# The router's products as fp32r with high and low parts side by side, and the second norm written over the tile of the input tokens

## The chip, the cores and the metric

The kernel runs on one core of a Trainium2 chip. What counts is the device time in microseconds of one execution. Before the change it is 1837.02 us, the median of three runs (1834.33 to 1839.08).

## The reference, cut to what matters

One layer over 1024 tokens of 1024 features. After the token mixing, its output projection with the gated residual, the second norm and the choice of tokens by 16 experts follow:

```python
y_x = (sigmoid(ga) * a + sigmoid(gb) * bb) @ w_out
x = x + g1 * y_x
h = modulate(rms_norm(x, norm2_g), sh2, sc2)          # (..)*(1+sc2) + sh2
aff = softmax((h @ w_router).astype(float32), axis=-1) # 1024 x 16
gate, idx = top_k(swapaxes(aff, 1, 2), 128)            # per expert: its 128 best tokens
xe = h[idx]                                            # gathered for each expert
```

Then each expert computes silu(xe @ w_gate) * (xe @ w_up) @ w_down for its 128 tokens, and a final norm closes. All is float32, and the choice of tokens depends on small differences in aff.

## The kernel before

Most products are done with operands that are split into a high part (rounded to fp32r) and a low part (the rest); three fp32r products, high x high, low x high and high x low, stand for one float32 product. `split` (L90 to L93) makes the two: a cast on ACT (L92), then a subtraction on DVE (L93). A few products are plain float32, the router's among them.

The stages follow each other: norms and the projection w_in, the scan, attention, the merge of the branches, the output projection with second norm and router (about 1079 to 1191 us), the search for the 128 best tokens per expert (to about 1216), the experts, the final norm. TensorE's (PE's) instructions run in the order in which the code writes them. DVE, ACT, POOL and the SP queue, which issues most DMAs, have their order from a scheduler that goes by due times and by `tc.high_priority`. Each engine's instructions run in their order, so one that waits holds up all that stand behind it.

The output projection works on eight tiles t of 128 tokens, each in four column quarters c of 256. For one (t, c) `y_mm` issues 24 fp32r products into the PSUM tile py. After two quarters `y_part` follows: x1 = py * g1 (L1083, DVE), x1 += xin, the input tokens (L1084, DVE), the squares' sum (L1085, ACT, which writes its unused elementwise result over xin). After the last quarter x1 goes to ACC, POOL computes the root r (L1089 to L1093), and `second_norm` writes h = x1 * r * s2 (L1100, DVE), adds sh2 (L1101) and sends h to the DRAM tensor H (L1102, SP), from which the experts gather. h has one buffer, xin two, x1 three, hT one.

The router doesn't read h: the norm's gain is multiplied into wr beforehand (`head2`, L968 to L973, in the merge stage), and r and the shift's part c0 are applied to the products. `x1_turn` transposes half of x1 (four blocks of 128x128) into pth and copies it to hT (L1109, ACT for the first half of a tile, DVE for the second). `router` runs eight float32 products of hT and wr, which have hT as weights and 16 columns (L1115), and the softmax's first steps (re, L1119; the maximum, L1120; exp, L1122; the reciprocal, L1123), raised in priority. `spread` scales into affb (ACT, L1133), transposes it (PE, L1135) and copies it to ar and aff.

For the last tiles `y_mm` and these small steps are interleaved by hand: `after` appends steps to the deque `turns`, and the table TN tells how many are taken behind each y_mm. So router(3) comes directly behind the transposes of its second half, router(5) as well, while router(0), (1), (2), (4) and (6) have one y_mm between; spread comes one or more y_mm behind its router. After the last y_mm TensorE has only the last transposes, router(7) and spread(7), and then the small products of the search.

pth, plg (the router's PSUM tile) and psp (spread's) share two PSUM banks. The tile aux, which POOL fills for the search (L1199 to L1206), has its own place.

Of the kernel before, what the change touches and what calls it, by code (L numbers as in the profile page):

```python
# [16 lines left out]
OP = mybir.AluOpType  # L17
# [4 lines left out]
D = 1024  # L22
# [23 lines left out]
def _layer(tc, nc, top, A, out):  # L46
# [9 lines left out]
    rt = top.enter_context(mkpool(name="rt", bufs=1))  # L56
# [185 lines left out]
    with ExitStack() as st:  # L242
        pool = st.enter_context(mkpool("right", name="pre", bufs=1))
        ps = st.enter_context(mkpool(name="preps", bufs=1, space=PSUM))
# [72 lines left out]
        for k in range(8):  # L317
            w2 = hx_pool.tile([128, 2, 2048], F32R, name="wm2", tag="hx1%d" % (k % 2))
            split(w2[:, 0], w2[:, 1], wm[k])
            for j in range(4):  # L320
                for i in range(2):
                    nc.tensor.matmul(pm[j], s4[:, k], w2[:, i, j * 512:(j + 1) * 512],
                                     start=(k == 0 and i == 0), stop=(k == 7 and i == 1))
# [14 lines left out]
        for j in range(16):  # L338
# [7 lines left out]
                                       op0=OP.add, op1=OP.mult)  # L346
# [42 lines left out]
    with ExitStack() as st:  # L389
        pool = st.enter_context(mkpool("right", name="sa", bufs=2))  # L390
# [39 lines left out]
        with tc.high_priority(offset=LK):  # L430
# [6 lines left out]
            r = pool.tile([128, 20], F32, name="kr_", bufs=1)  # L437
# [93 lines left out]
    with ExitStack() as st:  # L531
        pool = st.enter_context(mkpool("right", name="hg", bufs=1))
# [415 lines left out]
    with ExitStack() as st:  # L948
# [9 lines left out]
        nc.sync.dma_start(hd[8:], dram(sMod, 1024, [[128, 16], [1, 128]]))  # L958
        cols = rt.tile([128, 24], F32, name="cols")
        c0 = rt.tile([128, 16], F32, name="c0")  # L960

        def head():
            pv = ps.tile([128, 512], F32, name="pvc", tag="pth")
# [4 lines left out]
        def head2():  # L968
            pc = ps.tile([128, 512], F32, name="pc0", tag="pth")
            for k in range(8):  # L970
                nc.tensor.matmul(pc[:, :16], cols[:, 8 + k:9 + k].to_broadcast([128, 128]), wr[:, k], start=(k == 0), stop=(k == 7))
            nc.vector.tensor_copy(c0, pc[:, :16])
            nc.vector.tensor_tensor(wr, wr, cols[:, 16:, None].to_broadcast([128, 8, 16]), op=OP.mult)  # L973


        MG = [[[mp.tile([128, 4, 512], F32R, name="mg", tag="mg%d%d%d" % (i, c, n)) for n in range(2)] for c in range(2)] for i in range(2)]
# [72 lines left out]
        n2 = pool.tile([128, D], F32, name="n2", tag="xin", bufs=2)  # L1049
        nc.sync.dma_start(n2, dram(A["norm2_g"], 0, [[0, 128], [1, D]]))  # L1050
        nc.vector.scalar_tensor_tensor(row["s2"], row["s2"], 1.0, n2, op0=OP.add, op1=OP.mult)
        mats = pool.tile([128, 2, 128], F32, name="mats", tag="h", bufs=1)
        nc.scalar.dma_start(mats, A["c_mats"])
        nc.gpsimd.tensor_copy(tri, mats[:, 0])
        nc.gpsimd.tensor_copy(blk, mats[:, 1])
# [13 lines left out]
        X1 = {}  # L1069

        def y_part(t, c, nc_):

            ts, cs = slice(t * 128, (t + 1) * 128), slice(c * 256, (c + nc_) * 256)
            if c == 0:
                x = pool.tile([128, D], F32, name="xin", tag="xin", bufs=2)
                nc.sync.dma_start(x, A["x"][0, ts])
                x1 = pool.tile([128, D], F32, name="x1", tag="x1", bufs=3)
                ss = pool.tile([128, 4], F32, name="ss2", bufs=2)
                hT = pool.tile([128, 8, 128], F32, name="hT", tag="hT", bufs=1)
                X1[t] = [x, x1, ss, hT]  # L1080
            x, x1, ss, _ = X1[t]
            p = PY[t, c, "both"] if nc_ == 2 else PY[t, c]
            nc.vector.tensor_tensor(x1[:, cs], p, row["g1"][:, cs], op=OP.mult)  # L1083
            nc.vector.tensor_tensor(x1[:, cs], x1[:, cs], x[:, cs], op=OP.add)  # L1084
            nc.scalar.activation(x[:, cs], x1[:, cs], AF.Square, scale=1.0 / 32, accum_out=ss[:, c:c + 1])  # L1085
            if c + nc_ == 4:
                nc.sync.dma_start(ACC[ts], x1)
                m = pool.tile([128, 1], F32, name="r2m", tag="r2m", bufs=2)
                nc.gpsimd.tensor_scalar(m, ss[:, :1], ss[:, 2:3], EPS, op0=OP.add, op1=OP.add)  # L1089
                if nc_ == 1:  # L1090
                    nc.gpsimd.tensor_scalar(m, m, ss[:, 3:4], None, op0=OP.add)
                r = pool.tile([128, 1], F32, name="r2", tag="r2", bufs=2)
                nc.gpsimd.tensor_tensor(r, m, mhalf[:, :1], op=OP.pow)  # L1093
                X1[t].append(r)
                if t < 7:
                    second_norm(t, x1, r)

        def second_norm(t, x1, r):
            h = pool.tile([128, D], F32, name="h", tag="h", bufs=1)
            nc.vector.scalar_tensor_tensor(h, x1, r, row["s2"], op0=OP.mult, op1=OP.mult)  # L1100
            nc.vector.tensor_tensor(h, h, row["sh2"], op=OP.add)  # L1101
            nc.sync.dma_start(H[t * 128:(t + 1) * 128], h)  # L1102

        def x1_turn(t, c, nc_):
            _, x1, _, hT, *_ = X1[t]
            p = ps.tile([128, 4, 128], F32, name="pth", tag="pth")[:, :2 * nc_]
            for k in range(2 * nc_):
                nc.tensor.transpose(p[:, k], x1[:, (2 * c + k) * 128:(2 * c + k + 1) * 128], ident)
            (nc.vector.tensor_copy if c == 2 else nc.scalar.copy)(hT[:, 2 * c:2 * c + 2 * nc_], p)  # L1109

        def router(t):
            _, x1, _, hT, r = X1.pop(t)
            p = ps.tile([128, 512], F32, name="plg", tag="pth")[:, :16]
            for k in range(8):
                nc.tensor.matmul(p, hT[:, k], wr[:, k], start=(k == 0), stop=(k == 7))  # L1115
            m = pool.tile([128, 4], F32, name="rm", tag="rm", bufs=2)
            e = pool.tile([128, 16], F32, name="re", tag="re", bufs=2)
            with tc.high_priority(offset=100):
                nc.vector.scalar_tensor_tensor(e, p, r, c0, op0=OP.mult, op1=OP.add)  # L1119
                nc.vector.tensor_reduce(m[:, 0:1], e, axis=AX.X, op=OP.max)  # L1120
                nc.vector.tensor_scalar(m[:, 1:2], m[:, 0:1], -1.0, None, op0=OP.mult)
                nc.scalar.activation(e, e, AF.Exp, bias=m[:, 1:2], scale=1.0, accum_out=m[:, 2:3])  # L1122
                nc.vector.reciprocal(m[:, 3:4], m[:, 2:3])  # L1123
            EM[t] = e, m, x1, r

        EM = {}

        def spread(t):

            ab = pool.tile([128, 16, 8], F32, name="affb", tag="affb")  # L1130
            with tc.high_priority(offset=100):
                e, m, x1, r = EM.pop(t)
                nc.scalar.activation(ab, e[:, :, None].to_broadcast([128, 16, 8]), AF.Copy, scale=m[:, 3:4])  # L1133
                p = ps.tile([128, 512], F32, name="psp", tag="pth")[:, :128]
                nc.tensor.transpose(p, ab.rearrange("p e r -> p (e r)"), ident)  # L1135
                nc.vector.tensor_copy(ar16[:, t * 128:(t + 1) * 128], p.bitcast(U16)[:, 1::2])
                nc.scalar.copy(ar[:, t * 128:(t + 1) * 128], p)
                nc.scalar.copy(aff[:, t], ab[:, :, 0])
            if t == 7:
                second_norm(t, x1, r)  # L1140

        for k in ((0, 6), (6, 8)):
            for t in range(2):
# [48 lines left out]

    CAP = 128
    pos = rt.tile([128, 16, 8], BF, name="pos")
    aux = rt.tile([128, 8, 16, 5], BF, name="aux")
    with ExitStack() as st:
        pool = st.enter_context(mkpool(name="tk", bufs=1))
        ps = st.enter_context(mkpool(name="tkps", bufs=1, space=PSUM))
# [312 lines left out]
```

## Time and profile before

| | us |
|---|---|
| median of three runs | 1837.02 |
| profiled execution | 1835.68 |
| its span | 1833.9 |
| PE busy in the span | 1728.6 (94%) |
| DVE busy | 1325.1 (72%) |
| ACT busy | 981.6 (54%) |
| POOL busy | 225.1 (12%) |

The profile is one execution, taken on the core. The span runs from its first to its last instruction; the run around it is 1.8 us longer. Busy shares are means over stages with different limits: what a change in one stage is worth is read from that stage, by the order in which each engine works and by what ends its waits. PE is a matmul, PEld the load of its weights, which runs beside the matmul before; a float32 product leaves two records of each, an fp32r one a single record. fp32r operands appear as f32 in PE's rows. SPq is the SP engine issuing a DMA; its duration is that of the issue, and the time to landing stands elsewhere. A row of the timeline with x16 merges 16 like instructions, from the first's start to the last's end.

### The profile page before, as it was taken

How to read it: one execution, taken by the hardware profiler on the slowest of the kernel's cores; microseconds unless marked ns; L12 is line 12 of the kernel's file. 1: busy time of each engine (PE TensorE's matmuls, PEld its weight loads, DVE VectorE, ACT ScalarE, POOL GpSimd, SP SyncE). 2: the span in 40 equal slices, each digit the busy share in tenths (PEclk: the TensorE clock that was granted, in tenths of full speed). 3: DMA queues.
4: the chain of work that ended last, by engine and by line, in shares of the span. 5: the costliest groups of instructions: out<-in, count | busy, mean ns of one | idle time of the engine just before them, and what ended most of it. 6: DMA issues, size and time to landing. Idle time of an engine off the chain costs nothing. (4 is left out here: it accounts for less than half of the span.)

```text
span 1833.9 us, 26101 instructions
## 1 busy us (share of the span) xinstructions
PE 1728.6 (94%) x9819; PEld 1451.0 (79%) x9820; DVE 1325.1 (72%) x2016; ACT 981.6 (54%) x1608; POOL 225.1 (12%) x218
## 2 busy tenths in 40 slices
PE   5899999999999899999999999849999999999996
PEld 2799887899988678787777899838888888887774
DVE  5756322876756567777887664469999999999897
ACT  6522331332322367777767432237777777776665
POOL 3400001020000201111100010030010011001103
PEclk8899999999999999999999999969999999999998
DMA  8386445353332311101222676569999999999962
GB/s 321 98 290 238 155 144 186 128 159 106 128 113 81 119 51 34 53 24 58 94 91 99 223 269 230 176 238 356 380 380 375 382 385 369 383 384 381 357 244 95
DMA packets 206319, 383.87 MB, mean 209 GB/s; under 512 B 17488, under 2 KB 65568, under 8 KB 202864
## 3 DMA queue, kind: packets, MB, share of 16 engines
q1 hardware_dynamic: 194944, 360.92, 55.2%
q0 software_dynamic: 4832, 19.34, 3.9%
q10 hardware_dynamic: 6416, 1.94, 0.4%
q8 instruction: 77, 1.26, 0.3%
q14 instruction: 50, 0.41, 0.1%
HBM read 323.02 MB, written 59.13 MB: 208 GB/s over the span
## 5 line engine op out<-in xcount | busy, mean ns | idle before, releaser
L93 DVE TENSOR_TENSOR elo<-eraw,ehi 128x1024 fp32r<-128x1024 f32 x378 | 452.1, 1220 | 22.4 <-ACT ehi L92 14.9
L92 ACT CAST ehi<-eraw 128x1024 fp32r<-128x1024 f32 x384 | 383.7, 1048 | 86.5 <-PE pgu L178 48.4
L177 PE MATMUL pgu<-elo,xeT 128*128 128x512 f32 x512 | 203.5, 397 | 2.8 <-DVE elo L93 2.4
L176 PE MATMUL pgu<-ehi,xeT 128*128 128x512 f32 x512 | 205.3, 401 | 0.2 <-ACT xeT L92 0.2
L178 PE MATMUL pgu<-ehi,xeT 128*128 128x512 f32 x512 | 201.6, 394 | 0.0
L176 PE MATMUL pj<-hx,whi 128*128 128x512 f32 x448 | 185.7, 414 | 6.2 <-ACT stg L567 4.2
L178 PE MATMUL pj<-hx,wlo 128*128 128x512 f32 x448 | 176.4, 394 | 0.0
L177 PE MATMUL pj<-hx,whi 128*128 128x512 f32 x448 | 175.9, 393 | 0.0
L797 ACT ACTIVATE p<-s,m,qsc 128x512 f32<-128x512 f32 (+1 forms) x192 | 134.2, 711 | 18.8 <-DVE m L794 18.6
L790 DVE TENSOR_REDUCE m<-s 128x1 f32<-128x512 f32 (+1 forms) x192 | 104.2, 595 | 43.8 <-PE s L788 43.6
L176 PE MATMUL pj<-whi,hx 128*128 128x256 f32 x448 | 130.9, 292 | 3.8 <-DVE stg L541 1.9
L92 ACT CAST pT<-ptp 128x512 fp32r<-128x512 f32 x160 | 92.4, 593 | 75.4 <-PE ptp L806 75.2
L178 PE MATMUL pj<-whi,hx 128*128 128x256 f32 x448 | 128.1, 286 | 1.4 <-DVE hx L93 1.3
L93 DVE TENSOR_TENSOR pT<-ptp,pT 128x512 fp32r<-128x512 f32 x160 | 108.0, 684 | 26.5 <-ACT pT L92 25.6
L177 PE MATMUL pj<-wlo,hx 128*128 128x256 f32 x448 | 127.2, 284 | 0.0
L177 PEld LDWEIGHTS pgu<-elo,xeT 128*128 128x128 f32 x512 | 96.2, 188 | 28.6 <-DVE elo L93 8.1
L178 PEld LDWEIGHTS pgu<-ehi,xeT 128*128 128x128 f32 x512 | 96.1, 188 | 23.1 <-DVE xeT L93 0.4
L176 PEld LDWEIGHTS pgu<-ehi,xeT 128*128 128x128 f32 x512 | 96.7, 189 | 22.1 <-ACT xeT L92 0.5
L176 PE MATMUL pye<-ehi,hdT 128*128 128x512 f32 x256 | 105.3, 411 | 0.0
L816 PE MATMUL pv<-pT,vs 128*128 128x512 f32 x320 | 102.9, 404 | 1.8 <-DVE pT L93 1.5
L177 PE MATMUL pye<-elo,hdT 128*128 128x512 f32 x256 | 102.3, 400 | 1.2 <-DVE elo L93 1.2
L176 PEld LDWEIGHTS pj<-hx,whi 128*128 128x128 f32 x448 | 85.2, 190 | 21.1 <-ACT stg L567 5.1
(367 smaller groups left out, 3788.7 us busy)
## 6 DMA issues: line engine op xcount, KB each, us to landing
eraw<-in_w_exp_gate SPq DMA_DIRECT2D x64, 1024.0 KB, 10.0
eraw<-in_w_exp_up SPq DMA_DIRECT2D x64, 1024.0 KB, 9.5
eraw<-in_w_exp_down SPq DMA_DIRECT2D x64, 1024.0 KB, 10.0
wm<-in_w_mod SPq DMA_DIRECT2D x24, 1024.0 KB, 6.3
raw<-in_w_in SPq DMA_DIRECT2D x21, 1024.0 KB, 6.7
sFK<-sg SPq DMA_DIRECT2D x32, 256.0 KB, 2.3
sGT<-stg SPq DMA_DIRECT2D x32, 256.0 KB, 2.0
F<-sFK SPq DMA_DIRECT2D x8, 640.0 KB, 4.2
```

The source lines that it names most:

```text
L92: nc.scalar.copy(hi, src)
L93: (eng or nc.vector).tensor_tensor(lo, src, hi.bitcast(F32), op=OP.subtract)
L176: nc.tensor.matmul(p, a[0](k), b[0](k), start=s, stop=False)
L177: nc.tensor.matmul(p, a[0](k), b[1](k), start=False, stop=False)
L178: nc.tensor.matmul(p, a[1](k), b[0](k), start=False, stop=e)
L790: nc.vector.tensor_reduce(m[:, a:a + 1], s, axis=AX.X, op=OP.max)
L797: nc.scalar.activation(p, ss[a], AF.Exp, bias=m[:, 7:8], scale=sc, accum_out=SU[t, g][:, a, h:h + 1])
L816: nc.tensor.matmul(PV[t, g].rearrange("p a b -> p (a b)"), VS[:, g, j], hl[i], start=(j == 0 and i == 0), stop=(j == 9 and i == 1))
```

## The change

The router's weights are split once, behind the multiplication by the gain, into wr2, where the 16 high and the 16 low columns lie side by side. hT holds a high and a low part of x1's transposes, made by `split` in place of the copy. Each k then has two fp32r products: high hT with all 32 columns, and low hT with the 16 high columns, which adds to the first half. `re` becomes two instructions on DVE, one for each half of the columns.

The tile h goes: `second_norm` writes into xin, and H is sent from there. A later load into that buffer of xin so has to wait for the transfer to H. hT is twice as large, mats moves to its tag, and aux shares its place with wr2.

```diff
@@ head2
             nc.vector.tensor_tensor(wr, wr, cols[:, 16:, None].to_broadcast([128, 8, 16]), op=OP.mult)
+            split(wr2[:, :, :16], wr2[:, :, 16:], wr)
...
-        mats = pool.tile([128, 2, 128], F32, name="mats", tag="h", bufs=1)
+        mats = pool.tile([128, 2, 128], F32, name="mats", tag="hT", bufs=1)
...
-                hT = pool.tile([128, 8, 128], F32, name="hT", tag="hT", bufs=1)
+                hT = pool.tile([128, 2, 8, 128], F32R, name="hT", tag="hT", bufs=1)
...
-        def second_norm(t, x1, r):
-            h = pool.tile([128, D], F32, name="h", tag="h", bufs=1)
+        def second_norm(t, h, x1, r):
             nc.vector.scalar_tensor_tensor(h, x1, r, row["s2"], op0=OP.mult, op1=OP.mult)
...
-            (nc.vector.tensor_copy if c == 2 else nc.scalar.copy)(hT[:, 2 * c:2 * c + 2 * nc_], p)
+            split(hT[:, 0, 2 * c:2 * c + 2 * nc_], hT[:, 1, 2 * c:2 * c + 2 * nc_], p)
...
             for k in range(8):
-                nc.tensor.matmul(p, hT[:, k], wr[:, k], start=(k == 0), stop=(k == 7))
+                nc.tensor.matmul(p, hT[:, 0, k], wr2[:, k], start=(k == 0), stop=False)
+                nc.tensor.matmul(p[:, :16], hT[:, 1, k], wr2[:, k, :16], start=False, stop=(k == 7))
...
-                nc.vector.scalar_tensor_tensor(e, p, r, c0, op0=OP.mult, op1=OP.add)
+                nc.vector.scalar_tensor_tensor(e, p[:, :16], r, c0, op0=OP.mult, op1=OP.add)
+                nc.vector.scalar_tensor_tensor(e, p[:, 16:], r, e, op0=OP.mult, op1=OP.add)
...
-    aux = rt.tile([128, 8, 16, 5], BF, name="aux")
+    aux = rt.tile([128, 8, 16, 5], BF, name="aux", tag="aux")
```

The calls of `second_norm` pass xin (x) along. The scheduler orders the engines anew. PE's order is the same but for the router's products. Line numbers of the changed kernel are up to four higher. The first place is the SP queue at the start of the stage: the loads of the input tokens (xin) between the transfers of tiles 0 to 2 to ACC and H, first before.

```order
L1087 DMA ACC<-x_10570 128x1024
L1102 DMA H<-h 128x1024
L1087 DMA ACC<-x_10602 128x1024
L1076 DMA xin<-in_x 128x1024 x2
L1102 DMA H<-h 128x1024
```

The same place now:

```order
L1089 DMA ACC<-x_10573 128x1024
L1103 DMA H<-xin 128x1024
L1089 DMA ACC<-x_10605 128x1024
L1078 DMA xin<-in_x 128x1024
L1103 DMA H<-xin 128x1024
L1078 DMA xin<-in_x 128x1024
```

The two loads, issued together before, now have the second transfer to H between them, and each goes to a buffer from which a transfer to H is sent ahead of it.

The second place is DVE from tile 6's first columns of its second half (x_11371, now x_11423) to the router of tile 5 (re), first before.

```order
L1083 TENSOR_TENSOR x_11371<-py,g_10431 128x512
L1109 COPY hT<-pth 128x512
L1084 TENSOR_TENSOR x_11371<-x_11371,xin 128x512
L1119 SCALAR_TENSOR_TENSOR re<-plg,r_11286,c_9991 128x16
L1120 TENSOR_REDUCE rm<-re 128x1
L1121 TENSOR_SCALAR rm<-rm 128x1
L1100 SCALAR_TENSOR_TENSOR h<-x_11371,r_11467,s_10435 128x1024
L1123 RECIPROCAL rm<-rm 128x1
L1101 TENSOR_TENSOR h<-h,sh_10433 128x1024
```

And now:

```order
L1085 TENSOR_TENSOR x_11423<-py,g_10434 128x512
L1086 TENSOR_TENSOR x_11423<-x_11423,xin 128x512
L93 TENSOR_TENSOR hT<-pth,hT 128x512
L1101 SCALAR_TENSOR_TENSOR xin<-x_11423,r_11530,s_10438 128x1024
L1122 SCALAR_TENSOR_TENSOR re<-plg,r_11328,c_9991 128x16
L1102 TENSOR_TENSOR xin<-xin,sh_10436 128x1024
L1123 SCALAR_TENSOR_TENSOR re<-plg,r_11328,re 128x16
L1124 TENSOR_REDUCE rm<-re 128x1
L1125 TENSOR_SCALAR rm<-rm 128x1
L1127 RECIPROCAL rm<-rm 128x1
```

The norm of tile 6 stood between the maximum and the reciprocal of tile 5's router; now its first instruction stands ahead of re and its second between re's two halves.

The third place is DVE after the last y_mm, for tile 7, first before.

```order
L1084 TENSOR_TENSOR x_11543<-x_11543,xin 128x256
L1109 COPY hT<-pth 128x256
L1100 SCALAR_TENSOR_TENSOR h<-x_11543,r_11637,s_10435 128x1024
L1119 SCALAR_TENSOR_TENSOR re<-plg,r_11637,c_9991 128x16
L1101 TENSOR_TENSOR h<-h,sh_10433 128x1024
L1120 TENSOR_REDUCE rm<-re 128x1
```

And now:

```order
L1086 TENSOR_TENSOR x_11607<-x_11607,xin 128x256
L93 TENSOR_TENSOR hT<-pth,hT 128x512
L1101 SCALAR_TENSOR_TENSOR xin<-x_11607,r_11711,s_10438 128x1024
L93 TENSOR_TENSOR hT<-pth,hT 128x256 x2
L1102 TENSOR_TENSOR xin<-xin,sh_10436 128x1024
L1122 SCALAR_TENSOR_TENSOR re<-plg,r_11711,c_9991 128x16
L1123 SCALAR_TENSOR_TENSOR re<-plg,r_11711,re 128x16
L1124 TENSOR_REDUCE rm<-re 128x1
```

The norm's first instruction stood behind the last copy to hT; now the subtractions that make the low part of the last two quarters stand behind it, and the norm's second instruction ahead of re.

## Rows read from the trace of the kernel before

**Rows 1.** The page of the profile, its first line
```profile
span 1833.9 us, 26101 instructions
```

**Rows 2.** Busy us by stretch: engine busy (xinstructions), then PEclk, DMA share, GB/s
```profile
1020.00:1060.00 40.00, 40.00 (x185) 33.14 (x184) 28.96 (x43) 19.61 (x26) 0.00 (x0) 1.00 0.83 276
1156.00:1168.00 12.00, 11.86 (x104) 11.76 (x102) 5.89 (x13) 2.39 (x8) 0.00 (x0) 1.00 0.19 75
1180.00:1192.00 12.00, 7.02 (x54) 6.18 (x55) 6.53 (x17) 4.24 (x16) 2.43 (x6) 0.88 0.82 289
1300.00:1500.00 200.00, 200.00 (x932) 161.70 (x931) 190.89 (x212) 149.84 (x168) 22.25 (x11) 1.00 1.05 377
```

**Rows 3.** TensorE's waits, 1095 to 1192: total us, times, longest us
```profile
PE psp L1135 <- ACT affb L1133: 4.2, 3, 2.8
...
PE plg L1115 <- DVE hT L1109: 0.3, 1, 0.3
```

**Rows 4.** Timeline of tile 0's stretch: start us, us, instruction [idle before <-releaser]
```profile
1096.57 0.33 SPq L1102 DMA_DIRECT2D H<-h  x1
...
1098.31 1.23 SPq L1076 DMA_DIRECT2D xin<-in_x  x2
...
1101.38 1.28 DVE L1100 SCALAR_TENSOR_TENSOR h<-x,r,s 128x1024 f32<-128x1024 f32 x1 [3.51 <-DMA H<-h]
...
1104.31 0.69 DVE L1084 TENSOR_TENSOR x<-x,xin 128x512 f32<-128x512 f32 x1
...
1105.65 1.86 PEld L1115 LDWEIGHTS plg<-wr,hT 128*128 128x128 f32 x16 [0.19 <-DVE hT L1109]
...
1107.65 0.23 DVE L1119 SCALAR_TENSOR_TENSOR re<-plg,r,c 128x16 f32<-128x16 f32 x1 [1.25 <-PE plg L1115]
```

**Rows 5.** Timeline of weight loads (PEld) in the scan, 345 to 349
```profile
344.96 1.76 PEld L612 LDWEIGHTS psc<-Z,kc 128*128 128x128 f32 x15
```

**Rows 6.** Groups of weight loads by shape: busy us, mean ns | idle before
```profile
L178 PEld LDWEIGHTS pj<-hx,wlo 128*128 128x128 f32 x448 | 84.6, 189 | 18.5
...
L1115 PEld LDWEIGHTS plg<-wr,hT 128*128 128x128 f32 x128 | 15.1, 191 | 1.0 <-DVE hT L1109 1.0
```

**Rows 7.** Timeline of the first gathers' weight loads (PEld)
```profile
1226.74 0.57 PEld L1298 LDWEIGHTS <-oh 128*128 128x128 bf16 x8 [0.27 <-issue]
```

**Rows 8.** Tile h, the transfers that read it
```profile
DMA to landing us min/median/max: 2.6/3.1/7.6
```

**Rows 9.** DMA issues: count, KB each, median us to landing
```profile
xin<-in_x SPq DMA_DIRECT2D x8, 512.0 KB, 5.8
```

**Rows 10.** The page's costliest groups, two rows of 512 columns from PSUM
```profile
L92 ACT CAST pT<-ptp 128x512 fp32r<-128x512 f32 x160 | 92.4, 593 | 75.4 <-PE ptp L806 75.2
...
L93 DVE TENSOR_TENSOR pT<-ptp,pT 128x512 fp32r<-128x512 f32 x160 | 108.0, 684 | 26.5 <-ACT pT L92 25.6
```

**Rows 11.** Timeline of tile 5's end, 1165 to 1174
```profile
1168.70 0.23 DVE L1119 SCALAR_TENSOR_TENSOR re<-plg,r,c 128x16 f32<-128x16 f32 x1 [0.56 <-PE plg L1115]
...
1169.97 1.29 DVE L1100 SCALAR_TENSOR_TENSOR h<-x,r,s 128x1024 f32<-128x1024 f32 x1 [0.65 <-POOL r L1093]
...
1171.82 0.33 PE L1135 MATMUL psp<-ident,affb 128*128 128x128 f32 x1 [0.24 <-ACT affb L1133]
```

**Rows 12.** Timeline of tile 7's end, 1182 to 1193
```profile
1185.56 1.86 PEld L1115 LDWEIGHTS plg<-wr,hT 128*128 128x128 f32 x16 [0.53 <-DVE hT L1109]
...
1186.26 1.28 DVE L1100 SCALAR_TENSOR_TENSOR h<-x,r,s 128x1024 f32<-128x1024 f32 x1 [0.76 <-POOL r L1093]
...
1188.84 0.16 DVE L1120 TENSOR_REDUCE rm<-re 128x1 f32<-128x16 f32 x1
...
1190.31 0.48 PE L1135 MATMUL psp<-ident,affb 128*128 128x128 f32 x1 [2.79 <-ACT affb L1133]
```

**Rows 13.** Stretches around two gaps of TensorE, columns as in the second group
```profile
460.00:462.00 2.00, 0.33 (x3) 0.14 (x1) 0.82 (x4) 0.59 (x1) 1.30 (x2) 1.00 0.64 161
1189.00:1190.00 1.00, 0.00 (x0) 0.00 (x0) 0.32 (x2) 0.55 (x3) 0.00 (x0) 0.59 0.34 135
```

More of the change, by code (lines that the diff above doesn't have):

```diff
@@ L960, in _layer @@
         c0 = rt.tile([128, 16], F32, name="c0")
+        wr2 = rt.tile([128, 8, 32], F32R, name="wr2", tag="aux")
         def head():
@@ L1095, in y_part @@
                 if t < 7:
-                    second_norm(t, x1, r)
-        def second_norm(t, x1, r):
-            h = pool.tile([128, D], F32, name="h", tag="h", bufs=1)
+                    second_norm(t, x, x1, r)
+        def second_norm(t, h, x1, r):
             nc.vector.scalar_tensor_tensor(h, x1, r, row["s2"], op0=OP.mult, op1=OP.mult)
@@ L1108, in x1_turn @@
                 nc.tensor.transpose(p[:, k], x1[:, (2 * c + k) * 128:(2 * c + k + 1) * 128], ident)
-            (nc.vector.tensor_copy if c == 2 else nc.scalar.copy)(hT[:, 2 * c:2 * c + 2 * nc_], p)
+            split(hT[:, 0, 2 * c:2 * c + 2 * nc_], hT[:, 1, 2 * c:2 * c + 2 * nc_], p)
         def router(t):
-            _, x1, _, hT, r = X1.pop(t)
-            p = ps.tile([128, 512], F32, name="plg", tag="pth")[:, :16]
+            x, x1, _, hT, r = X1.pop(t)
+            p = ps.tile([128, 512], F32, name="plg", tag="pth")[:, :32]
             for k in range(8):
-                nc.tensor.matmul(p, hT[:, k], wr[:, k], start=(k == 0), stop=(k == 7))
+                nc.tensor.matmul(p, hT[:, 0, k], wr2[:, k], start=(k == 0), stop=False)
+                nc.tensor.matmul(p[:, :16], hT[:, 1, k], wr2[:, k, :16], start=False, stop=(k == 7))
             m = pool.tile([128, 4], F32, name="rm", tag="rm", bufs=2)
@@ L1123, in router @@
                 nc.vector.reciprocal(m[:, 3:4], m[:, 2:3])
-            EM[t] = e, m, x1, r
+            EM[t] = e, m, x, x1, r
         EM = {}
@@ L1131, in spread @@
             with tc.high_priority(offset=100):
-                e, m, x1, r = EM.pop(t)
+                e, m, x, x1, r = EM.pop(t)
                 nc.scalar.activation(ab, e[:, :, None].to_broadcast([128, 16, 8]), AF.Copy, scale=m[:, 3:4])
@@ L1139, in spread @@
             if t == 7:
-                second_norm(t, x1, r)
+                second_norm(t, x, x1, r)
         for k in ((0, 6), (6, 8)):
```

## The prediction

> **What bounds the kernel now.** First the span: 1833.9 us [rows 1]. The profiled execution as a whole took 1835.68 us, 1.8 more, and the median of the runs shown is 1837.02. The sum below is a difference in microseconds, made in the span, and added to the median.
>
> Second, the busy time by stretch, because the change works in one stage, the output projection with the router (about 1079 to 1191 us). The reader is to see three things in it [rows 2]. While the norm's gain goes into wr (1020 to 1060 us), TensorE is busy 40.00 of 40 us, DVE 28.96, ACT 19.61. In the middle of the stage TensorE is busy 11.86 of 12 us (104 records, 114 ns each), DVE only 5.89 and ACT 2.39: TensorE bounds, and an added DVE instruction costs nothing unless TensorE waits for it. At the stage's end (1180 to 1192) TensorE falls to 7.02 of 12 us: there a chain over DVE and ACT bounds. Last, 1300 to 1500 us, in the experts, TensorE is busy 200.00 of 200 us. So what the router stage loses or wins shifts all later work by as much; there is no slack behind it to swallow a delay.
>
> Third, TensorE's waits in the stage [rows 3]: 4.2 us in three waits for affb (2.8 of it after the last router), 0.3 for the hT of tile 0. Little is to be won here beyond the router's own products, and much can be added.
>
> **Part 1, the router's products.** Before, eight f32 products per tile are 16 records; a tile's 16 loads take 1.86 us, the last of them 0.19, so (1.86 - 0.19)/15 = 111 ns apart [rows 4]. After, there are eight products of 32 columns and eight of 16, as fp32r; I count one record each, 16 again. Does a column cost? The scan's f32 products with another shape (15 loads in 1.76 us, 112 ns apart [rows 5]) come at the same rate, so the load sets the pace. An fp32r load of 128x128 lasts 189 ns, the router's f32 load 191 [rows 6]. No row shows an fp32r product with so few columns, so I bound it: above by the 114 ns of the projection's 256-column products [rows 2], below by the gathers' bf16 loads, eight in 0.57 us, (0.57 - 0.19)/7 = 54 ns [rows 7]. I take 112, since the 189 is next to the 191 and far from bf16; part 1 then gives 0. By the lower bound it gives 16 x 0.057 = 0.9 us per router.
>
> The Trainium skill (page "TensorE: Matmul & The Clock Gate", section "Weight-path perf modes — Fast Weight Load (FWL) and DoubleRow") says that loads of 128 weights go in a fast mode where the input isn't FP32. If fp32r counts as FP32 there, the sum is as I make it; if not, the routers gain, which is the first rival. The trace agrees so far that bf16 loads come at twice the pace of f32 ones.
>
> **Part 2, xin as the norm's target.** Before, the second h of the stage waits 3.51 us for the first H transfer, whose landing frees the tile [rows 4]; this goes. But TensorE didn't wait for it: DVE's next product there reads py of tile 2, which TensorE itself finishes only a microsecond later. In exchange the load of xin(2), which stands behind H(0) on the SP queue, must now wait until H(0) has landed, and ACC(1), H(1), xin(3) stand behind it or next to it. H(0) is issued at 1096.57 [rows 4]. The landing took 4.81 us there, 2.6 at least and 3.1 in the median [rows 8]; a load of xin 5.8 [rows 9], with two of them issued together [rows 4], which the change pulls apart. I bound x1 += xin at 1101.8 (2.6 + 2.6) and 1107.2 (4.8 + 5.8) and take 1103.3, in the lower half, because H(0) now goes without the two loads beside it; with py of tile 2 as late as now, DVE could not come to it much sooner. Before, it began at 1104.31 [rows 4].
>
> From 1103.3: addition 0.7, Square and its read-out 0.8 (ACT's order puts the cast behind it), cast 0.59, subtraction 0.68 [rows 10], small gaps, so TensorE may load at 1106.2 where it did at 1105.65: **+0.6** (bounds +0.2, where the load is early and only the cast is added, and +4.5).
>
> **Part 3, one cast and one subtraction in place of a copy.** Each half tile costs ACT 593 ns and DVE 684 [rows 10] in series, 1.3 us where a copy took 0.6 to 0.7. TensorE notices it where the router follows its last transposes closely. In tile 3 it follows at once: the low half of the products gives 8 x 0.112 = 0.9 us of cover, the data come 1.35 us after, so 0.45 is bare, **+0.4**. Tile 5 has the same, but what follows covers it. The others have 24 products (2.7 us at 114 ns) between, 0; in tiles 2 and 4, where DVE is then a little later for the next tile's r and for affb, I add **+0.2** together, an estimate. The second small STT (0.23 us [rows 4]) is on no path but the tail's.
>
> Tile 5. Here DVE's order changes: the STT of h(6) and its addition now stand before the two STT of re(5), or between them. Before, re ran at 1168.70, ahead of h(6) at 1169.97, and the transpose of affb at 1171.82 [rows 11]. After, h(6) starts some 0.5 us earlier, since x1 += xin no longer stands behind a copy: 1169.45. Then 1.2 for it, 0.25 for the first STT, 1.2 for h's addition: the second STT at 1172.1, the maximum at 1172.4. From the maximum to the transpose the tail's rows give 1190.31 - 1188.84 = 1.47 [rows 12], so 1173.8: **+2.0**. TensorE's list has the next 24 products behind this transpose, all stand. If DVE comes to h(6) late enough for re(5), the cost is 0, the lower bound.
>
> **Part 4, the tail.** DVE's order is: h(7)'s STT (r is ready at 1186.26 as before, 1.28 long [rows 12]), then the subtractions of the last two quarters, then h's addition, re twice, the maximum. Router(7), which started at 1185.56 [rows 12], now needs the subtraction behind the STT: 1187.54 + 0.4 = 1187.94. From a router's first load to re takes 1107.65 - 1105.65 = 2.0 us [rows 4]: re 1189.94, second STT and maximum at 1190.37, against 1188.84: **+1.5**. Behind it stands everything: the search for the thresholds, then the experts.
>
> TensorE now stands 2.4 us ahead of router(7), after a stretch that already had gaps. In the trace the granted clock reads 0.59 in the slice that ends such a gap at 1189 to 1190, but 1.00 after a dense stretch at 460 to 462 [rows 13]. I take it that it falls to the 1.2 GHz level before router(7), twice as long as now, 16 x 0.111 = **+1.8**; the bounds are 0 and 1.8.
>
> **The rest costs nothing**: the split of wr (a cast and a subtraction of a quarter of the size of [rows 10], at most 0.6 us together) lies in the merge stage beside TensorE's 40.00 of 40 us, with DVE idle for 11 of them [rows 2], and its first reader is 65 us later; uncovered it would cost its 0.6. The casts into aux, moved behind router(7) on POOL, end before aff arrives. The expert loads keep their order but for one.
>
> **Sum:** 0 + 0.6 + 0.4 + 0.2 + 2.0 + 1.5 + 1.8 = +6.5 us on the profiled execution; on the median 1837.0 + 6.5 = 1843.5.
>
> **The rivals.** A difference of 0.3%, 5.5 us, is about what a measurement of this kernel can tell from no change.
>
> First, on the other side: fp32r loads come at the bf16 pace. Five routers gain 0.9 us each (tiles 0, 1, 2, 4, 6: 4.5), tile 3 0.4, tile 5 nothing, since DVE bounds it, the tail about 0.6: -5.5, in all +1, not slower beyond what is told; it decides from a pace under about 75 ns. For it: a product is then one record, as a bf16 one is, and not two as in f32. Against it: 189 beside 191. 0.12, and 0.06 for a gain beyond 5.5, where the waits of tile 5 and the tail don't arise either (0.6 + 0.4 + 0.2 - 5.5 is -4.3, and an unseen gain with it).
>
> Second: the clock stays high before router(7), or DVE serves re(5) in time. 6.5 - 1.8 = +4.7 or 6.5 - 2.0 = +4.5: within 0.3%. For it: 1.00 at 460 to 462. Against it: the stretch before 1185 is not dense. 0.24.
>
> Third: H(0) lands late, and xin(2) takes 5.8 behind it: +4.5 in place of 0.6, in all +10.4. For it: the 4.81 measured. Against it: that landing shared the engines with two loads. 0.13.
>
> The forecast, +6.5 with its own range of +4.5 to +9, has the remaining 0.45, of which 0.02 lie within 0.3%.
>
> **Numbers.** Slower 0.43 + 0.13 = 0.56; same 0.12 + 0.24 + 0.02 = 0.38; faster 0.06. The range leaves out half of the late case and the gain: 1836.5 to 1849.5.
>
> **What will show it.** Router spans of 1.8 to 1.9 us and loads of about 190 ns confirm part 1; half of that is the first rival. TensorE's wait for affb in tile 5 of some 2 us confirms the order on DVE. In the tail, router(7) near 1188 on the old scale, waiting for DVE, its 16 records 3.6 us long and a granted clock about 0.5 from 1187 on. In tile 0 the addition of xin ends on a DMA wait; whether that ends before 1104 tells the third rival. I am wrong if TensorE's waits in the stage don't grow by at least 3 us, or if the experts, dense after, don't carry the shift to the end.

## The result, and the profile after

The changed kernel takes 1846.35 us, the median of seven runs (1844.21 to 1851.84), beside 1837.99 for the kernel before (seven runs, 1834.33 to 1839.08): 8.4 us more. The ratio is 1.0054, its 95% interval 1.0042 to 1.0067, so 7.7 to 12.3 us slower. Forecast were 1843.5 us, 6.5 more. The span of the profiled execution answers to [rows 1]:

```profile
span 1843.8 us, 26135 instructions
```

Of the 9.9 us between the spans 7.7 lie in the router's stage. I measure it from TensorE's first transposes of tile 0 to the search's first product: 97.12 us before, 104.83 after, +7.7. The marks between them, the routers' first loads (r0, r5, r7) and the transposes of affb (p0 to p7), cut it into pieces. Each number in this table is the difference of two start times on the timelines of weight loads (the last of each row ends at the search's first product):

| us | to r0 | r0 to p0 | p0 to p2 | p2 to p3 | p3 to r5 | r5 to p5 | p5 to r7 | r7 to p7 | p7 to search | stage |
|---|---|---|---|---|---|---|---|---|---|---|
| before | 10.09 | 7.77 | 29.19 | 8.60 | 15.18 | 5.44 | 13.74 | 4.75 | 2.37 | 97.12 |
| changed | 11.21 | 9.00 | 29.61 | 9.11 | 15.31 | 7.34 | 16.12 | 4.75 | 2.37 | 104.83 |
| a2_again | 11.07 | 9.03 | 29.61 | 9.08 | 15.31 | 7.33 | 16.13 | 4.06 | 2.37 | 103.99 |
| a3_again | 10.73 | 8.97 | 29.61 | 9.11 | 15.31 | 7.34 | 16.08 | 4.19 | 2.38 | 103.71 |
| e1_router | 9.83 | 8.13 | 27.82 | 9.12 | 16.09 | 7.09 | 15.62 | 4.95 | 3.79 | 102.44 |
| e2_norm | 9.84 | 7.78 | 29.21 | 8.59 | 15.18 | 5.43 | 13.74 | 4.75 | 2.37 | 96.90 |
| e4_late0 | 12.68 | 7.50 | 26.74 | 9.11 | 15.30 | 7.33 | 16.09 | 5.63 | 2.37 | 102.75 |
| e5_fill0 | 12.47 | 7.45 | 29.61 | 9.08 | 15.30 | 7.33 | 16.12 | 4.25 | 2.37 | 103.96 |
| e6_fix5 | 11.34 | 7.49 | 29.61 | 9.08 | 15.31 | 6.92 | 16.33 | 4.69 | 2.38 | 103.14 |
| e7_tail | 11.91 | 10.59 | 29.58 | 9.12 | 15.30 | 7.34 | 14.32 | 5.10 | 2.47 | 105.73 |
| e8_all | 12.68 | 7.50 | 26.73 | 10.34 | 15.49 | 5.97 | 14.29 | 5.10 | 2.46 | 100.57 |
| e9_fill | 11.02 | 7.44 | 29.61 | 10.62 | 15.30 | 7.32 | 16.11 | 4.01 | 2.22 | 103.65 |
| e10_best | 9.83 | 7.78 | 29.36 | 8.57 | 15.15 | 5.44 | 13.74 | 4.84 | 2.47 | 97.17 |

In the changed kernel, tile 0 lost 1.12 us up to its router and 1.23 behind it, tiles 1 to 4 some 1.1 in all, tile 5 1.9, and the tail 2.4. TensorE's waits in the stage, on the changed kernel's lines, answer to [rows 3]:

```profile
PE psp L1139 <- ACT affb L1137: 3.5, 2, 2.1
PE plg L1117 <- DVE hT L93: 3.2, 2, 2.2
PE plg L1118 <- DVE hT L93: 1.2, 2, 0.7
PE pth L1109 <- ACT ar L1141: 0.8, 1, 0.8
```

The waits of the router's products for DVE (hT), 0.3 us before, are now 4.4, in tile 0, tiles 3 and 5, and the tail. The 0.8 for ACT are not new: the same transposes, those of tile 7, waited 0.7 us for ACT before. The router itself answers to [rows 6]; the two groups are its 32-column and its 16-column products:

```profile
L1118 PEld LDWEIGHTS plg<-wr,hT 128*128 128x128 f32 x64 | 12.8, 200 | 1.4 <-DVE hT L93 1.4
L1117 PEld LDWEIGHTS plg<-wr,hT 128*128 128x128 f32 x64 | 12.7, 198 | 3.7 <-DVE hT L93 3.7
```

A load takes 198 to 200 ns in the mean (191 before). Where none waits and the clock is high, the sixteen start 1.67 us apart from first to last in both kernels: 111 ns each. The stretches, columns as in [rows 2], are behind router(0), at the tail, and in the experts:

```profile
1110.00:1114.00 4.00, 4.00 (x22) 4.00 (x22) 2.74 (x7) 2.61 (x5) 0.85 (x2) 0.57 0.36 135
1192.00:1202.00 10.00, 3.77 (x21) 3.12 (x21) 5.84 (x14) 3.46 (x9) 3.78 (x9) 0.69 0.97 316
1300.00:1500.00 200.00, 200.00 (x940) 161.71 (x939) 191.15 (x216) 149.62 (x168) 24.54 (x12) 1.00 1.05 377
```

The reader is to see 0.57 in the first: behind router(0) the granted clock fell for most of the stretch to the 1.2 GHz level, with TensorE busy 4.00 of 4 us; from router(0) to the transpose of its affb it took 9.00 us, where the five runs below with a high clock there take 7.44 to 7.50. In the experts TensorE is busy 200 of 200 us as before, so that nothing there takes the shift up: what follows the stage lasts 641.2 us before and 642.0 now. Tile 0, answering to [rows 4]:

```profile
1098.29 0.33 SPq L1103 DMA_DIRECT2D H<-xin  x1
...
1101.97 0.33 SPq L1078 DMA_DIRECT2D xin<-in_x  x1
...
1105.48 0.69 DVE L1086 TENSOR_TENSOR x<-x,xin 128x512 f32<-128x512 f32 x1 [0.95 <-DMA xin<-in_x]
...
1106.25 0.63 ACT L1087 ACTIVATE xin<-x 128x512 f32<-128x512 f32 x1 [5.94 <-DVE x L1086]
...
1106.88 0.57 ACT L92 CAST hT<-pth 128x512 fp32r<-128x512 f32 x1
...
1107.48 0.69 DVE L93 TENSOR_TENSOR hT<-pth,hT 128x512 fp32r<-128x512 f32 x1 [1.31 <-ACT hT L92]
...
1108.23 0.19 PEld L1117 LDWEIGHTS plg<-wr,hT 128*128 128x128 f32 x1 [1.25 <-DVE hT L93]
```

xin(2) is loaded 3.7 us after H(0) is issued, and the addition ends a wait for it. Then the four steps stand one behind another: addition, Square on ACT, the cast that ACT has behind Square, the subtraction, and only then router(0), after 1.25 us of waiting. The addition itself is not late: it begins 8.46 us behind the stage's start, and before the change it began at 8.75 [rows 4], since DVE then waited 3.51 us for the landing of H(0). Tile 5, answering to [rows 11]:

```profile
1174.38 1.28 DVE L1101 SCALAR_TENSOR_TENSOR xin<-x,r,s 128x1024 f32<-128x1024 f32 x1 [1.23 <-POOL r L1095]
...
1175.59 0.23 DVE L1122 SCALAR_TENSOR_TENSOR re<-plg,r,c 128x16 f32<-128x16 f32 x1
...
1175.73 1.22 DVE L1102 TENSOR_TENSOR xin<-xin,sh 128x1024 f32<-128x1024 f32 x1
...
1176.86 0.23 DVE L1123 SCALAR_TENSOR_TENSOR re<-plg,r,re 128x16 f32<-128x16 f32 x1
...
1178.61 0.15 PEld L1139 LDWEIGHTS psp<-ident,affb 128*128 128x128 f32 x1 [0.43 <-ACT affb L1137]
```

h(6) on DVE stands ahead of the first re and between the two, and the transpose of affb comes 4.23 us after h(6)'s start; before, 1.85. The tail, answering to [rows 12]:

```profile
1193.05 1.28 DVE L1101 SCALAR_TENSOR_TENSOR xin<-x,r,s 128x1024 f32<-128x1024 f32 x1 [0.98 <-POOL r L1095]
1194.26 0.75 DVE L93 TENSOR_TENSOR hT<-pth,hT 128x256 fp32r<-128x256 f32 x2
1194.73 0.19 PEld L1117 LDWEIGHTS plg<-wr,hT 128*128 128x128 f32 x1 [2.40 <-DVE hT L93]
...
1197.99 0.17 DVE L1124 TENSOR_REDUCE rm<-re 128x1 f32<-128x16 f32 x1
...
1199.48 0.48 PE L1139 MATMUL psp<-ident,affb 128*128 128x128 f32 x1 [2.06 <-ACT affb L1137]
```

The subtractions stand behind h(7)'s first instruction, and router(7) waits 2.40 us.

### The profile page after: what moved, and what is told of

Its sections match the earlier page's. It is cut to its first block, busy times and chain, and to the rows that moved or that the text cites. A ratio compares the mean times of both kernels' runs of the same rounds, so it can differ in the third digit from the quotient of the medians.

```text
span 1843.8 us, 26135 instructions
## 1 busy us (share of the span) xinstructions
PE 1735.0 (94%) x9819; PEld 1456.9 (79%) x9820; DVE 1332.1 (72%) x2034; ACT 987.8 (54%) x1617; POOL 225.0 (12%) x218
```

## The experiments

Low and high clock mean the two levels of the granted clock, 1.2 and 2.4 GHz. Ratios are to the kernel before, with 95% intervals. Theory A is that of the prediction, widened by what the changed kernel's trace shows at tile 0. Of every run there is one profile, so a place of the low clock is that of one execution.

**The router alone.**
```diff
@@ e1_router, from the changed kernel
-            nc.vector.scalar_tensor_tensor(h, x1, r, row["s2"], ...)
+            for cs in (slice(0, 512), slice(512, 1024)):
+                h = pool.tile([128, 512], F32, name="h", tag="h", bufs=1)
+                nc.vector.scalar_tensor_tensor(h, x1[:, cs], r, row["s2"][:, cs], ...)
...
-    pos = rt.tile([128, 16, 8], BF, name="pos")
+    pos = consts.tile([128, 16, 8], BF, name="pos", tag="masks")
```


> Only the fp32r router; the norm has its own tile h again (in two halves of 512 columns, since a whole one doesn't fit beside the larger hT; pos shares wr's place). Stage = from TensorE's first transposes of tile 0 to the search's first product: 97.1 us before, 104.8 in the changed kernel. Theory A (cast and subtraction in series ahead of the router's products, and the granted clock that falls behind each of the stalls, make the loss): 104.8 +- 1, total 7 to 10 us over before, low clock behind router(0) or behind router(3) or router(5) as in the changed kernel. Theory B (the load of xin behind the transfer to H makes tile 0's loss of 1.1 us and the 1.2 us of low clock behind it): 102.3 +- 0.7.

Measured: 1.0018 (1.0002 to 1.0035), stage 102.44. Router(0) doesn't wait, though it has the casts:

```profile
1098.47 0.75 DVE L1103 SCALAR_TENSOR_TENSOR h<-x,r,s 128x512 f32<-128x512 f32 x1 [0.30 <-DMA H<-h]
...
1101.92 0.69 DVE L1086 TENSOR_TENSOR x<-x,xin 128x512 f32<-128x512 f32 x1 [1.36 <-DMA xin<-in_x]
...
1103.92 0.69 DVE L93 TENSOR_TENSOR hT<-pth,hT 128x512 fp32r<-128x512 f32 x1 [1.31 <-ACT hT L92]
...
1104.81 0.19 PEld L1119 LDWEIGHTS plg<-wr,hT 128*128 128x128 f32 x1
```

The addition comes 6.94 us behind the stage's start, 1.5 earlier than in the changed kernel, and the same chain ends ahead of TensorE: the casts cost nothing there. But this run is not the router's change alone. With h in halves DVE waits only 0.30 us for the landing of H, where the kernel before waited 3.51, so its addition is 1.8 us earlier than in the kernel before as well (8.75). What the casts cost with the addition at that place it doesn't test. The stage fits B's number, but by sums of this edit's own. From p0 to p2 it takes 1.8 us less than the changed kernel, since spread(2) no longer waits; from p7 to the search it takes 1.4 more, where the second half of h(7) now stands on DVE ahead of the search's first count.

**The norm alone.**
```diff
@@ e2_norm, from the kernel before
-                    second_norm(t, x1, r)
+                    second_norm(t, x, x1, r)
...
-        def second_norm(t, x1, r):
-            h = pool.tile([128, D], F32, name="h", tag="h", bufs=1)
+        def second_norm(t, h, x1, r):
...
```


> Only the norm over xin; the router is the float32 one with a single copy. Theory A: x1 += xin of tile 2 begins within 0.5 us of where it did (8.75 us behind the stage's start), router(0) doesn't wait, the clock stays high to the search: stage 97.1 +- 0.5, total within 0.3% of before. Theory B: router(0) stands about 1 us and the clock falls behind it: stage 98.2 to 99.5, total 1 to 2.5 us over before.

Measured: 0.999 (0.9974 to 1.0007), stage 96.90, the clock high up to the last router, as before.

```profile
1104.32 0.69 DVE L1084 TENSOR_TENSOR x<-x,xin 128x512 f32<-128x512 f32 x1 [1.14 <-DMA xin<-in_x]
...
1104.93 0.68 DVE L1108 COPY hT<-pth 128x512 f32<-128x512 f32 x1
...
1105.69 0.97 PEld L1114 LDWEIGHTS plg<-wr,hT 128*128 128x128 f32 x8
```

The addition waits for xin as in the changed kernel, 8.46 us behind the start in both, but only one copy follows it, and router(0) is on time. B falls: the norm over xin alone costs nothing. So it is the steps behind the addition, Square, cast and subtraction, that make router(0) late. In all five profiles where router(0) waits for them (the changed kernel's three, e6_fix5 and e7_tail) its first load comes 2.74 to 2.75 us behind the addition, wherever that lies between 7.98 and 9.17.

Whether the new place of the norm has a share in tile 0's loss is not shown. With the addition at the 8.75 us of the kernel before, the same steps would bring router(0) to 11.50, an estimate; no run has the fp32r router beside the old norm, whose whole tile h doesn't fit beside the larger hT.

**Router(0) later.**
```diff
@@ e4_late0, from the changed kernel
+                if t == 0:
+                    turns.extend([lambda: None, lambda: router(t), lambda: None])
+                    return
...
         def x1_turn(t, c, nc_):
+            if (t, c) == (1, 2):
+                spread(0)
```


> The changed kernel, with router(0) 24 products later in TensorE's order and spread(0) 24 products later as well; all other places are unchanged. Theory A (the stall at router(0) costs its 1.1 us and then 1.2 us by the low clock that follows it): no low clock at 13 to 17 us of the stage, spread(0) apart all later marks 2.3 us earlier, stage 102.5 +- 0.5. Rival C (the low clock at 1110 is not of the stall, it comes at some time in each run): 103.7, with a stretch of low clock somewhere in the stage's middle all the same.

Measured: 1.0026 (1.0008 to 1.0045), stage 102.75, as theory A has it. The stretch in which the low clock fell before, and the one with router(7):

```profile
1106.00:1118.00 12.00, 12.00 (x105) 12.00 (x104) 7.77 (x15) 5.10 (x12) 0.86 (x2) 1.00 0.38 133
1190.00:1194.00 4.00, 3.53 (x16) 3.49 (x16) 1.88 (x4) 0.00 (x0) 0.00 (x0) 0.50 0.98 353
```

In the first TensorE is busy throughout and its clock stays at 1.00. Router(7) starts 2.4 to 3.0 us earlier than in the three profiles of the changed kernel. But then the clock falls in its wait: its sixteen loads take 3.15 us from first to last, and r7 to p7 5.63, which gives part of the gain back.

**Products ahead of router(0).**
```diff
@@ e5_fill0, from the changed kernel; pd is the whole PSUM tile of plg
+            if t == 0:
+                for k in range(12):
+                    nc.tensor.matmul(pd[:, :256], MG[0][0][0][:, k % 4, :128], WO[0][0][:, k % 8], start=True, stop=True)
```


> The changed kernel, with twelve products of 256 columns ahead of router(0)'s, whose result is overwritten: some 1.3 us in which TensorE would stand otherwise. Theory A (a stall leads to the low clock): router(0) ends at the same place or up to 0.3 us later, but no low clock follows, so stage 103.5 +- 0.5. Rival C (the low clock has another cause, and the products are plain added work): stage 104.8 to 106.2, low clock as before.

Measured: 1.0032 (1.0018 to 1.0046), stage 103.96. The edit did not do what it should: plg's bank came free only when the subtraction ended, so the twelve products stood behind the 1.0 us of waiting, not in it. Nevertheless no low clock followed:

```profile
1111.30 1.68 PE L1119 MATMUL plg<-whi,mg 128*128 128x256 f32 x12 [0.96 <-DVE hT L93]
...
1111.00:1123.00 12.00, 11.70 (x100) 11.70 (x101) 6.79 (x14) 4.60 (x11) 0.86 (x2) 1.00 0.38 138
```

From router(0) to p0 it takes 7.45 us for 9.00, which makes up for the 1.4 us of added work: p0 comes at 19.92 us, in the changed kernel's profiles at 19.70 to 20.21. (The stage is 0.9 us shorter than in the first of those, about as long as in the other two.) So a stall of 1.0 us was not always followed by the low clock. That the narrow products right behind the stall are what brings it fits this run, but one profile doesn't show it, and in e6_fix5 below they follow a stall without it.

**Products in both stalls, in a bank of their own.**
```diff
@@ e9_fill, from the changed kernel
+            if t in (0, 7):
+                pd = ps.tile([128, 512], F32, name="pd", tag="pb1")
+                for k in range(20 if t else 10):
+                    nc.tensor.matmul(pd[:, :256], MG[0][0][0][:, k % 4, :128], WO[0][0][:, k % 8], start=True, stop=True)
```


> The changed kernel, with ten products of 256 columns ahead of router(0) and twenty ahead of router(7), into a PSUM tile of their own that nobody reads: TensorE works in the two stalls and starts the routers when it did. Theory A (the low clock comes of stalls): no low clock between 1100 and router(7)'s end but perhaps in tile 5, router(7)'s 16 loads 1.67 us apart in all instead of 2.26, psp(0) 1.2 us earlier, stage 102.7 to 103.5. Rival C (the clock falls at its own times): low clock in the stage's middle as in the changed kernel, stage 104 to 105.5.

Measured: 1.0040 (1.0020 to 1.0059), stage 103.65.

```profile
1111.00:1123.00 12.00, 12.00 (x105) 12.00 (x104) 6.16 (x13) 5.20 (x12) 0.85 (x2) 1.00 0.46 169
1154.00:1158.00 4.00, 4.00 (x23) 4.00 (x23) 0.95 (x5) 1.02 (x4) 0.00 (x0) 0.57 0.00 0
```

With TensorE at work ahead of router(0), the clock behind it stays at 1.00 (r0 to p0 7.44 us for 9.00). Less was filled than meant: the addition came at 7.61 us here, so that router(0) would have started at 10.36 by the 2.75 above, and the ten products held it up to 11.02. Router(7) runs at the high clock (r7 to p7 4.01), but so it does without the products in two of the changed kernel's three profiles, so that shows nothing. And the clock falls behind router(3), whose loads have a gap of 0.5 us, and p2 to p3 takes 1.5 us more. A had no low clock there, and the stage is just over its range; C had one in the stage's middle, but the stage is under its range. The run doesn't decide between them.

**h(6) behind router(5)'s maximum.**
```diff
@@ e6_fix5, from the changed kernel
-                if t < 7:
+                if t == 6:
+                    r6 = pool.tile([128, 1], F32, name="r6", bufs=1)
+                    nc.gpsimd.tensor_scalar(r6, EM[5][1][:, 0:1], 0.0, r, op0=OP.mult, op1=OP.add)
+                    second_norm(t, x, x1, r6)
+                elif t < 7:
                     second_norm(t, x, x1, r)
```


> The changed kernel, with h(6) held back on DVE until the maximum of router(5) is there (its factor r comes out of an added POOL instruction that reads that maximum times zero). Theory A (tile 5's 1.9 us are made by DVE's order, h(6) ahead of and between the two re; the low clock that reads there in the changed kernel costs nothing): from router(5)'s first load to spread(5) 7.34 us before the edit, 5.7 to 6.2 now, stage 103.0 to 103.7 by this alone. Rival D (the low clock behind router(5)'s stall makes most of it): 7.0 to 7.4 where the clock falls there, and 5.5 to 6 only where it doesn't.

Measured: 1.0048 (1.0031 to 1.0066), stage 103.14, r5 to p5 6.92 us, between the two ranges. The rows are router(0)'s first load, the stretch behind it, and tile 5:

```profile
1109.00 0.19 PEld L1121 LDWEIGHTS plg<-wr,hT 128*128 128x128 f32 x1 [1.39 <-DVE hT L93]
...
1109.00:1121.00 12.00, 12.00 (x102) 12.00 (x103) 6.75 (x14) 5.09 (x12) 0.86 (x2) 1.00 0.43 160
1174.00:1178.00 4.00, 4.00 (x23) 4.00 (x22) 2.82 (x6) 1.02 (x4) 0.27 (x1) 0.57 0.02 4
```

The clock fell in tile 5, where TensorE's 24 products now bound. Inconclusive by itself; the stage is in A's range, but only because no low clock fell behind router(0). That is the second thing to see: router(0) waits 1.39 us, longer than in the changed kernel, its narrow products follow at once, and the clock stays high.

**h(7) behind router(7)'s maximum.**
```diff
@@ e7_tail, from the changed kernel
             if t == 7:
+                r7 = pool.tile([128, 1], F32, name="r7", bufs=1)
+                nc.gpsimd.tensor_scalar(r7, m[:, 0:1], 0.0, r, op0=OP.mult, op1=OP.add)
-                second_norm(t, x, x1, r)
+                second_norm(t, x, x1, r7)
```


> The changed kernel, with h(7) held back in the same way until the maximum of router(7). Theory A (the tail's 2.4 us are the subtractions behind h(7)'s first instruction): router(7)'s first load 1.5 to 1.9 us earlier against router(6)'s (9.47 us behind it in the changed kernel, 7.09 before), the transpose of affb 1.2 to 2.4 earlier, stage 102.4 to 103.6. Rival (cast and subtraction in series make it): router(7) at most 0.5 us earlier.

Measured: 1.0057 (1.0037 to 1.0077), stage 105.73.

```profile
1193.94 0.98 DVE L93 TENSOR_TENSOR hT<-pth,hT 128x256 fp32r<-128x256 f32 x2 [0.38 <-ACT hT L92]
...
1194.42 0.19 PEld L1117 LDWEIGHTS plg<-wr,hT 128*128 128x128 f32 x1 [0.60 <-DVE hT L93]
...
1197.02 0.17 DVE L1124 TENSOR_REDUCE rm<-re 128x1 f32<-128x16 f32 x1
```

Router(7) starts 7.67 us behind router(6) for 9.47, 1.8 earlier: A. p5 to p7 is 1.45 shorter than in the first profile of the changed kernel, where the low clock fell in router(7), and 0.8 shorter than in the other two, where it didn't; the rest is given back, because the reciprocal now stands behind h(7)'s first instruction. The stage missed its range by 2.1 us, since router(0) came 0.7 later and the low clock behind it lasted longer (r0 to p0 10.59).

**All three edits.** Those of e4_late0, e6_fix5 and e7_tail in one kernel.

> The changed kernel with three edits: router(0) and spread(0) 24 products later, h(6) behind the maximum of router(5), h(7) behind that of router(7). Theory A: the three gains add, 102.75 less 1.4 less 1.2 to 2.4: stage 98.9 to 100.2, total within 0.3% of before. Rival E (something that runs through the whole stage, such as the added work on DVE and ACT, takes over): no lower than 101.5.

Measured: 1.0029 (1.0016 to 1.0043), stage 100.57, 0.4 over A's range, since the low clock fell behind router(3) here (p2 to p3 10.34, 1.2 more), and under rival E's 101.5. Tile 5, with a high clock there:

```profile
1171.99 0.17 DVE L1130 TENSOR_REDUCE rm<-re 128x1 f32<-128x16 f32 x1
...
1172.64 1.28 DVE L1105 SCALAR_TENSOR_TENSOR xin<-x,r,s 128x1024 f32<-128x1024 f32 x1 [0.30 <-POOL r L1099]
...
1173.85 0.16 DVE L1133 RECIPROCAL rm<-rm 128x1 f32<-128x1 f32 x1
...
1174.49 0.33 PE L1145 MATMUL psp<-ident,affb 128*128 128x128 f32 x1
```

The maximum comes ahead of h(6), and r5 to p5 takes 5.97 us for 7.34, within A's 5.7 to 6.2. With the profiles that follow, that settles what e6_fix5 left open.

**The changed kernel again, twice.**

> The changed kernel once more, unedited, for another profile. If its stalls bring the low clock in some executions and not in others: router(0) 11.2 +- 0.3 us behind the stage's start as before, router(3) and router(5) with the same gaps of 0.5 to 0.8 us among their loads, but the low clock behind another of the three, or behind none; stage 103.6 to 105.5. If the place of the low clock belongs to the kernel: behind router(0) and in tile 5, as in the first profile, stage 104.8 +- 0.2.

> The changed kernel a third time, unedited. The same two expectations: with the place of the low clock by chance, stage 103.6 to 105.5 and another pattern of low clock than one of the two profiles; with a fixed place, stage 104.8 +- 0.2 and low clock behind router(0).

Measured: 1841.34 and 1845.72 us (single runs), stages 103.99 and 103.71. The low clock lies behind router(0) both times; of the first of them, with the transpose of tile 5's affb:

```profile
1109.00:1113.00 4.00, 4.00 (x23) 4.00 (x22) 3.26 (x7) 1.96 (x6) 0.85 (x2) 0.58 0.12 46
...
1176.40 0.33 PE L1139 MATMUL psp<-ident,affb 128*128 128x128 f32 x1 [1.49 <-ACT affb L1137]
```

r0 to p0 is 9.03 and 8.97. In tile 5 it doesn't recur, and r5 to p5 is still 7.33 and 7.34, so rival D falls: the low clock there cost nothing, because TensorE waits for affb anyway, 1.49 us with the high clock and 0.13 where its products ahead ran at the low one. In router(7) it hardly recurs either. Neither expectation holds in full: one place recurs, two don't.

**The shortest stage.** The norm over xin with the float32 router, and the edit of e7_tail.

> The norm over xin with the float32 router and a single copy (as e2_norm), and h(7) held back until the maximum of router(7): what the runs point to as the shortest stage. Theory A (tail: DVE no longer runs h(7) ahead of re and the maximum): the maximum about 1 us earlier, but the reciprocal stands behind h(7)'s first instruction, so the transpose of affb 0.3 to 0.7 us earlier; stage 96.3 to 96.7, against 96.9 of e2_norm and 97.1 before; the total not to be told from before (0.998 to 1.000). Rival: the reciprocal waits as long as the maximum gains: stage 96.9 to 97.3.

Measured: 1.0007 (0.9994 to 1.0021), stage 97.17: the rival.

```profile
1187.42 0.17 DVE L1119 TENSOR_REDUCE rm<-re 128x1 f32<-128x16 f32 x1
...
1188.07 1.28 DVE L1099 SCALAR_TENSOR_TENSOR xin<-x,r,s 128x1024 f32<-128x1024 f32 x1 [0.30 <-POOL r L1140]
1189.28 0.15 DVE L1122 RECIPROCAL rm<-rm 128x1 f32<-128x1 f32 x1
...
1189.92 0.47 PE L1134 MATMUL psp<-ident,affb 128*128 128x128 f32 x1 [2.88 <-ACT affb L1132]
```

The maximum stands at once behind re, but the reciprocal waits for h(7)'s first instruction, and p7 comes no earlier. No version beat the kernel before.

## Why the prediction was right, and where its terms were off

The time lies in the range and on the forecast side; the terms add up to 6.5, the stage shows 7.7, 6.9 and 6.6 in three profiles.

**Part 1, 0: right.** Sixteen loads, 111 ns apart before and after. The first rival falls: fp32r with so few columns doesn't come at the bf16 pace of [rows 7]. (That pace is 58 ns: a bf16 load lasts 164 ns in the mean, and my 54 took the last one to be as long as a float32 load.) The Trainium skill (page "TensorE: Matmul & The Clock Gate", section "Weight-path perf modes — Fast Weight Load (FWL) and DoubleRow") gives the fast mode to loads of 128 weights whose input isn't FP32, and doesn't say which of the two fp32r is; here it loads at the float32 pace.

**Tile 0, +0.6: the mechanism held, the size was off.** It cost 1.8 to 2.4 us (the first two columns of the table). The addition came 8.46 us behind the stage's start; I had 1103.3 - 1095.56 = 7.74, so 0.7 too early: H(0) was issued 0.3 later in its stage, and its landing and the load of xin took 7.2 us together, where I had 6.7. The chain behind it was as worked out, 2.75 us where I had 2.9. Missing was the low clock that follows, which I had weighed at the tail alone: 1.5 us against a high clock, 1.2 against the kernel before. The wait of xin for H(0), from which I started, is there, but in this profile the addition comes no later by it than before; the loss is that of the steps behind the addition.

**Tiles 1 to 4, +0.6 together: 1.1 measured.** Tile 3 gave 0.5 for 0.4; p0 to p2 gave 0.4 where I had 0.2, and p3 to r5 0.1.

**Tile 5, +2.0: right, 1.9**, and by the order on DVE, as e8_all shows.

**The tail, +1.5 and +1.8: the order right, the clock too dear.** Router(7) starts 2.38 us later in its piece, as worked out, and held back, h(7) lets it start 1.8 earlier (e7_tail). p5 to p7 grew by 2.4, 1.7 and 1.8 us in the three profiles: the order makes 1.7, and the low clock in router(7) 0.7 in one of three, not 1.8, since it fell in the middle of the router or behind it. Where it does fall ahead of router(7), as in e4_late0, it costs about what I had: r7 to p7 takes 5.63 us, for 4.06 and 4.19 in the two profiles with the high clock. So the price was nearly right, and the sum counted as certain what happens in some executions.

So the sum came out near because one term was too small by 1.2 to 1.8 and another too large by 0.9 to 1.6; that the two nearly cancel is luck. The third rival (xin at its latest) didn't come: the load landed before 1105.48 - 1097.02 = 8.46 us, not at 11.6. The second came true in part, the clock at the tail staying high in two of three profiles, and yet tile 0's low clock took its place.

Of the signs I named, TensorE's waits in the stage grew by 3.5 us in the first profile (5.2 to 8.7), hardly over the 3 asked for, because its wait for affb in tile 5, which I expected at some 2 us, reads 0.13 behind products at the low clock; in the other two it is 1.5, and the waits grew by 4.9 and 4.7. The 0.3 us of [rows 3] is a wait of router(7), not of tile 0 as I read it; no term rests on it.

**What stays open.** The ratio says 7.7 to 12.3 us, the stage 6.6 to 7.7. What precedes the stage took 1094.96 to 1100.23 us in all profiles, whatever the kernel, and what follows it 640.4 to 644.3; one profile of the kernel before can't tell whether the change has a share in that. The two later runs of the changed kernel lie only 1.8 and 6.2 us over the 1839.52 us that the kernel before has in the median of the runs beside them. What decides behind which of the stalls the clock falls is not settled: e6_fix5 has tile 0's stall and no low clock behind it. The same holds far from this change. The gap of TensorE at 460 us, after which the clock stayed at 1.00 [rows 13], is there in e2_norm too, 1.68 us for 1.67, and there, as in e7_tail, the clock falls behind it:

```profile
459.74 1.20 PE L697 MATMUL pot<-ident,gl 128*128 128x128 f32 x4 [1.68 <-issue]
...
460.00:462.00 2.00, 2.00 (x10) 1.76 (x10) 0.41 (x2) 0.86 (x2) 0.00 (x0) 0.60 0.46 159
```

So the same gap at the same place of the program leaves the clock high in one execution and is followed by the low level in another.

## What to carry to other kernels

Price added steps together with the place at which they start: here one copy behind an addition at 8.46 us was harmless, Square, cast and subtraction were harmless behind one at 6.94, and the same three behind one at 8.46 left TensorE standing. Look at what stands behind a waiting instruction in its engine's order: the cast behind Square on ACT and the subtractions behind the norm on DVE cost more than their own durations. Where a product takes as long as its weight load, two fp32r products gain nothing on a float32 one that leaves two records. And a price that hangs on the clock is a chance as well as a sum: the same stall was followed by the low clock in some executions and not in others.

## What the runs showed of the hardware

A wait of router(0) of 0.8 to 2.0 us, with its 16 narrow products right behind it, was followed by the 1.2 GHz level in four of five profiles that had this (the changed kernel's three and e7_tail; not e6_fix5). The length of the wait doesn't decide it: 0.83 us was followed by the low level (a3_again), 1.39 was not (e6_fix5). r0 to p0 then took 9.0 us, and 10.6 in e7_tail, for 7.5 with the high clock. It was not seen in the one profile where 12 wide products stood between the wait and the router (e5_fill0), nor in the one where 10 filled the wait (e9_fill). Behind the gaps of 0.5 and 0.8 us in router(3) and router(5) it came in some of the ten profiles with the fp32r router, behind router(3) in two (e8_all, e9_fill) and behind router(5) in three (the first of the changed kernel, e1_router, e6_fix5). It is a loss only where TensorE bounds: in tile 5 of the changed kernel the same fall cost nothing. In router(7) of e4_late0, wholly at the low level, the loads started 210 ns apart for 111. An fp32r product of 32 or of 16 columns took 111 ns, as much as each of the two records of a float32 product of 16.
